# Gate transposes one token block later, pooling sums one group later, weights one block sooner, in a hybrid mLSTM encoder block

## The chip, the cores and the metric

The kernel runs on one core of one Trainium2 chip. The metric is the device time of one execution in microseconds (us). Five engines work side by side, each through its own queue in order: TensorE (PE, with its weight loads as PEld), VectorE (DVE), ScalarE (ACT), GpSimd (POOL) and SyncE (SP), which issues nearly all of the DMA transfers of the stretch in question.

## What is computed

One encoder block: a modulated RMSNorm, one input projection, an mLSTM scan in both directions over four heads, a multi-scale pooling group beside it, an output projection, and a squared-ReLU MLP. The change lies in the projection of the four pooling groups and of the gates. Of the reference, what matters here:

```python
proj = jnp.einsum('bsd,dp->bsp', h, w_in)                 # 2048 tokens x 2576 columns
q, k, v, o, gates, u = jnp.split(proj, cuts, axis=-1)     # u: 4 pooling groups of 128 channels
log_i = gates[:, 0] + b_igate[:, None, :, None]
log_f = jax.nn.log_sigmoid(gates[:, 1] + b_fgate[:, None, :, None])
b = jnp.cumsum(lf, axis=-1)                               # in each chunk of 128 tokens
m_new = jnp.maximum(b_last + m, jnp.max(g, axis=-1))      # running maximum over the 16 chunks
for gi, win in enumerate((2, 4, 8, 16)):                  # centred means of u, less the token itself
    means.append((p[:, hi] - p[:, lo]) / cnt[None, :, None])
mixed = jnp.stack(means, axis=2) - uf
mod = silu(c) @ w_ada + b_ada                             # 6 x 1024 modulation values
```

## The kernel before

Activations lie transposed in SBUF, 8 tiles of 128 channels by 512 tokens for each of four token blocks, split into a high and a low part (`Hh`, `Hl`). A column block of 128 output channels and 512 tokens is 24 matmuls (`col_mm`, lines 404 to 406: high by high, low by high, high by low, over 8 tiles of channels). In the text such a block is called c15_0: column block 15, token block 0.

The stage in question runs from about 134 us to 262 us. It goes over the pooling groups g = 3, 2, 1, 0 (column blocks 15, 14, 13, 12), four token blocks each. Five kinds of work are woven into it:

- **The gates** (`gate_rows`, a generator that is advanced once per token block by `next(gates, None)`): transposes of small matrices on TensorE, called gT, gL, gM, gC and gD by their PSUM tiles, with scans and copies on VectorE and exponentials on ScalarE between them. gL needs `g_last` from VectorE (lines 329 to 332), gM the rows of the running maximum (lines 342 to 349), gC the exponentials (lines 366 to 371), gD the decay (line 383).
- **Weights** (`col_weights`): a 512 KB load `wr`, a cast `wh` on ScalarE, and the low part `wl` on VectorE. They are asked for when token block 1 of the group before has been computed.
- **Pooling** (lines 445 to 458): after the four blocks of a group have been copied to `u`, VectorE forms the sums in one tile `s` with a single buffer: log2(window) additions over some 2050 columns, two small corrections and a subtraction; then four stores `yd` of 256 KB each. The next group's first sum overwrites `s`, so that it waits for those stores.
- **Folding of the output weights**: a 512 KB load `wor`, a scaling on VectorE (line 462), two matmuls `wof` (line 465), two copies and stores.
- **Modulation values** (`mod_col`): for each of 32 columns a 512 KB load `ada` and a multiply-and-sum on VectorE (line 117).

The loads `wr`, `wor` and `ada` share three buffers (`raw`); a load is issued when the tile that holds its buffer has been read for the last time, and SyncE issues loads and stores strictly in its own order. When the stage ends, head 0's keys follow: projections c4_3 to c4_0, each copied (`k`, line 486), transposed (`kn`), scaled (`kb`, `kf`, lines 497 and 498), and multiplied with values loaded from memory (`va`, line 484; `kvb`, line 508). The tiles of this part lie where the pooling tiles were, so `kb` and the load `va` wait for the last group's stores.

The order of instructions on each engine is made by a scheduler from the order of the program and readiness; `tc.keep_in_program_order(ins)` holds an instruction to its place in the program.

Of the kernel before, what the change touches and what calls it, by code (L numbers as in the profile page):

```python
# [8 lines left out]
F32 = mybir.dt.float32  # L9
# [3 lines left out]
ALU = mybir.AluOpType  # L13
# [13 lines left out]
WIN = (2, 4, 8, 16)  # L27
# [8 lines left out]
def block_kernel(ctx, tc, x, x_t, cb, w_ada, b_ada, g_mix, g_ffn, g_head, p_scale, w_col, w_vg,  # L36
# [273 lines left out]
    def gate_rows(pg):  # L310
        def gt(name, n=P):
            return pg.tile([P, n], F32, name=name)
        li, lf, b_, m_, t0 = gt("g_li"), gt("g_lf"), gt("g_b"), gt("g_m"), gt("g_t")
        ps = tp("gT")
        pe.transpose(ps[:, 0:P], G2[:, 0], ident)
        pe.transpose(ps[:, P:2 * P], G2[:, 1], ident)
        ve.tensor_scalar(li, ps[:, 0:P], bgate[:, 0:1], None, ALU.add)
        ve.tensor_scalar(lf, ps[:, P:2 * P], bgate[:, 1:2], None, ALU.add)
        sc.activation(t0, lf, AF.Abs)
        sc.activation(t0, t0, AF.Exp, scale=-1.0)  # L320
        sc.activation(t0, t0, AF.Ln, bias=1.0)
        ve.scalar_tensor_tensor(lf, lf, 0.0, t0, ALU.min, ALU.subtract)
        fw, bw = slice(0, 64), slice(64, 128)
        ve.tensor_tensor_scan(b_[fw], ones[fw], lf[fw], 0.0, ALU.mult, ALU.add)
        ve.tensor_tensor_scan(b_[bw, ::-1], ones[bw], lf[bw, ::-1], 0.0, ALU.mult, ALU.add)
        ve.tensor_tensor_scan(m_[fw], lf[fw], li[fw], NEG, ALU.add, ALU.max)
        ve.tensor_tensor_scan(m_[bw, ::-1], lf[bw, ::-1], li[bw, ::-1], NEG, ALU.add, ALU.max)
        lasts = gt("g_last", 2)
        ve.tensor_copy(lasts[fw, 0:1], b_[fw, P - 1:P])
        ve.tensor_copy(lasts[bw, 0:1], b_[bw, 0:1])  # L330
        ve.tensor_copy(lasts[fw, 1:2], m_[fw, P - 1:P])
        ve.tensor_copy(lasts[bw, 1:2], m_[bw, 0:1])
        yield
        ps = tp("gL")
        pe.transpose(ps[0:1, 0:P], lasts[:, 0:1], ident)
        pe.transpose(ps[0:1, P:2 * P], lasts[:, 1:2], ident)
        rows = pg.tile([1, 4, P], F32, name="g_rows")
        ve.tensor_copy(rows[:, 0:2, :], ps[0:1, 0:2 * P].rearrange("p (a n) -> p a n", a=2))
        gp.memset(rows[:, 3, :], 0.0)
        for h in range(H):  # L340
            r = slice(h * NT, (h + 1) * NT)
            ve.tensor_tensor_scan(rows[:, 2, r], rows[:, 0, r], rows[:, 1, r], 0.0, ALU.add, ALU.max)
            r = slice(64 + h * NT, 64 + (h + 1) * NT)
            ve.tensor_tensor_scan(rows[:, 2, r][:, ::-1], rows[:, 0, r][:, ::-1],
                                  rows[:, 1, r][:, ::-1], 0.0, ALU.add, ALU.max)
        r2 = rows[:, 2, :].rearrange("p (d h c) -> p d h c", d=2, h=H)
        r3 = rows[:, 3, :].rearrange("p (d h c) -> p d h c", d=2, h=H)
        ve.tensor_copy(r3[:, 0, :, 1:NT], r2[:, 0, :, 0:NT - 1])
        ve.tensor_copy(r3[:, 1, :, 0:NT - 1], r2[:, 1, :, 1:NT])
        yield  # L350
        ps = tp("gM")
        pe.transpose(ps[:, 0:1], rows[:, 3, :], ident[0:1, 0:1])
        mp = gt("g_mp", 1)
        ve.tensor_copy(mp, ps[:, 0:1])
        ve.scalar_tensor_tensor(m_, b_, mp, m_, ALU.add, ALU.max)
        u = lf
        v = li
        ve.tensor_tensor(v, li, b_, ALU.subtract)
        ve.tensor_tensor(u, b_, m_, ALU.subtract)
        for d in range(2):  # L360
            dma(ua_d[:, 0, d, :], u[64 * d:64 * d + 64])
        ul = gt("g_ul", 1)
        ve.tensor_copy(ul[fw], u[fw, P - 1:P])
        ve.tensor_copy(ul[bw], u[bw, 0:1])
        a = t0
        sc.activation(a, u, AF.Exp, bias=mp)
        for d in range(2):
            dma(ua_d[:, 1, d, :], a[64 * d:64 * d + 64])
        wk = b_
        sc.activation(wk, v, AF.Exp, bias=ul)  # L370
        sc.activation(m_, m_, AF.Exp, scale=-1.0)
        ve.tensor_copy(ul[fw], a[fw, P - 1:P])
        ve.tensor_copy(ul[bw], a[bw, 0:1])
        yield
        ps = tp("gC")
        pe.transpose(ps[:, 0:P], v, ident)
        pe.transpose(ps[:, P:2 * P], wk, ident)
        pe.transpose(ps[:, 2 * P:3 * P], m_, ident)
        ve.tensor_copy(vcol, ps[:, 0:P])
        ve.tensor_copy(wkcol, ps[:, P:2 * P])  # L380
        ve.tensor_copy(emcol, ps[:, 2 * P:3 * P])
        dd = gt("g_dd")
        ve.tensor_scalar(dd, ident, ul, None, ALU.mult)
        yield
        ps = tp("gD")
        pe.matmul(ps[:, 0:P], ones, dd, start=True, stop=True)
        ve.tensor_copy(decb, ps[:, 0:P])


    def col_weights(ci):  # L390
        r = raw(f"wr{ci}").rearrange("p (k n) -> p k n", k=KT)
        dma(r, w_col[ci])
        hh = wq.tile([P, KT, P], F32R, tag="whi", name=f"wh{ci}")
        hl = wq.tile([P, KT, P], F32R, tag="wlo", name=f"wl{ci}")
        sc.copy(hh, r)
        ve.tensor_tensor(hl, r, asf(hh), ALU.subtract)  # L396
        return hh, hl
# [17 lines left out]
    with tc.tile_pool(name="pu", bufs=2) as pu, tc.tile_pool(name="psU", bufs=2, space=PSUM) as psU:  # L415
        wpl = pu.tile([P, 4, P], F32, name="wpl", bufs=1)
        dma(wpl, w_pool)
        edgec = pu.tile([P, 64], F32, name="edgec", bufs=1)
        dma(edgec, edge)
        pgs = ExitStack()  # L420
        pg = pgs.enter_context(tc.tile_pool(name="pg", bufs=1))
        gates = gate_rows(pg)
        w = col_weights(15)
        for g in (3, 2, 1, 0):
            win = WIN[g]
            hw = win // 2
            u = pu.tile([P, T + 16], F32, tag="u", name=f"u{g}")
            gp.memset(u[:, 0:8], 0.0)
            gp.memset(u[:, T + 8:T + 16], 0.0)
            for b in range(NB):  # L430
                cg = col_mm(12 + g, b, w)
                while True:
                    try:
                        next(cg)
                    except StopIteration as e:
                        ps = e.value
                        break
                if b or g < 3:
                    next(gates, None)
                sc.copy(u[:, 8 + 512 * b:8 + 512 * b + 512], ps)  # L440
                if b == 1:
                    wn = col_weights(11 + g if g else 4)
            w = wn

            s = pu.tile([P, T + 16], F32, tag="s", name=f"s{g}", bufs=1)
            n = T + 15
            ve.tensor_tensor(s[:, 0:n], u[:, 0:n], u[:, 1:n + 1], ALU.add)
            d = 2
            while d < win:
                n -= d  # L450
                ve.tensor_tensor(s[:, 0:n], s[:, 0:n], s[:, d:n + d], ALU.add)
                d *= 2
            s = s[:, 8 - hw:8 - hw + T]
            ve.tensor_tensor(s[:, 0:8], s[:, 0:8], edgec[:, 16 * g:16 * g + 8], ALU.mult)
            ve.tensor_tensor(s[:, T - 8:T], s[:, T - 8:T], edgec[:, 16 * g + 8:16 * g + 16], ALU.mult)
            ve.scalar_tensor_tensor(s, s, 1.0 / win, u[:, 8:8 + T], ALU.mult, ALU.subtract)
            for b in range(NB):
                dma(y_d[b][:, 4 + g, :], s[:, 512 * b:512 * b + 512])

            wr = raw(f"wor{g}")  # L460
            dma(wr, w_o[4 + g])
            ve.tensor_scalar(wr, wr, pscale[:, g:g + 1], None, ALU.mult)
            for n in range(2):
                ps = psU.tile([P, 512], F32, tag="y", name=f"wof{g}_{n}")
                pe.matmul(ps, wpl[:, g], wr[:, 512 * n:512 * n + 512], start=True, stop=True)
                e = evt(f"woe{g}_{n}")[:, :512]
                sc.copy(e, ps)
                dma(wo_d[g][:, 512 * n:512 * n + 512], e)
            for j in MODS[g]:
                mod_col(j)  # L470
        pgs.close()
        for k in range(KT):
            ve.scalar_tensor_tensor(s2[:, k:k + 1], mod[:, 32 + k:33 + k], 1.0, gffn[:, k:k + 1],
                                    ALU.add, ALU.mult)


    with tc.tile_pool(name="ps_", bufs=2) as sp, tc.tile_pool(name="psS", bufs=1, space=PSUM) as psS:
# [223 lines left out]
        for h in range(H):  # L701
# [5 lines left out]
            n = 0  # L707
# [563 lines left out]
```

## Time and profile before

| | us |
|---|---|
| median of 3 runs | 2036.94 (2034.96 to 2037.42) |
| the profiled execution | 2039.14 |
| its span in the profile | 2037.1 |
| mean granted TensorE clock | 0.997 of full speed |

The profiled execution is 2.0 us longer than the span that the profile shows and 2.2 us above the median. All times in the rows are counted from the start of the span. A row of a timeline gives start, duration, engine, line, operation, tiles and shapes, how many alike, and in brackets how long the engine had been idle before and what ended that.

### The profile page before, as it was taken

The page shows a single profiled execution, that of the slowest core. Times are in us where ns is not written, and L with a number is a line of the kernel's source. Part 1 is how long each engine was busy: PE and PEld are TensorE (multiplying, and loading weights), DVE is VectorE, ACT ScalarE, POOL GpSimd, SP SyncE. Part 2 cuts the span into 40 slices and gives each one's busy share as a digit, 9 for nine tenths or more (in the row PEclk, how much of TensorE's full clock was granted, in tenths as well). Part 3 has the DMA queues.
Part 4 walks back from the last instruction along what each step waited for, and adds up shares of the span by engine and source line. Part 5 has one row for each costly group of instructions (what it writes and reads, how often), then busy time and mean ns, then how long its engine had stood idle before and what let it go on. Part 6 is the DMA issues. An engine that isn't in the chain of part 4 may idle for free.

```text
span 2037.1 us, 27780 instructions
## 1 busy us (share of the span) xinstructions
PE 1987.5 (98%) x9591; PEld 1658.5 (81%) x9591; DVE 1356.5 (67%) x2456; ACT 918.3 (45%) x1704; POOL 129.7 (6%) x353
## 2 busy tenths in 40 slices
PE   7999999989999999999999999999999999999998
PEld 6997777778887888888888888888888888888886
DVE  6638636676646777555666766666877667768876
ACT  4721223333335668755556655556324224324432
POOL 1100012222210111000000000000000000000011
PEclk9999999999999999999999999999999999999999
DMA  8736867787548799765666766766887657648553
GB/s 339 237 108 209 285 205 220 253 254 226 180 131 271 236 270 315 209 196 182 224 203 224 228 226 215 226 206 225 280 268 257 225 156 262 224 158 275 187 165 132
DMA packets 298574, 452.87 MB, mean 222 GB/s; under 512 B 23569, under 2 KB 163137, under 8 KB 298306
## 3 DMA queue, kind: packets, MB, share of 16 engines
q1 hardware_dynamic: 228546, 413.35, 62.3%
q10 hardware_dynamic: 69888, 37.76, 6.1%
q8 instruction: 75, 1.23, 0.2%
q14 instruction: 65, 0.53, 0.1%
HBM read 290.40 MB, written 160.62 MB: 221 GB/s over the span
## 4 chain that ended last, share of the span: by engine, by line
PE 84%; DMA 7%; DVE 4%; issue 1%; ACT 1%; POOL 1%; SPq 1%; POOLq 0%; DVEq 0%; ACTq 0%
PE c L405 4%; PE c L404 4%; PE c L406 4%; DMA ua<-uad 1%; DMA ada<-in_w_ada 1%; DVE ada L117 1%; DMA wotd<-os 1%; DMA rob<-wotd 1%; DMA vraw<-in_w_v 1%; PE f000x L845 1%; PE o11x L845 1%; PE o10x L845 1%; PE o13x L845 1%; PE o03x L845 1%; PE o12x L845 1%
## 5 line engine op out<-in xcount | busy, mean ns | idle before, releaser
L404 PE MATMUL c<-Hh,wh 128*128 128x512 f32 x512 | 211.0, 412 | 0.0
L405 PE MATMUL c<-Hl,wh 128*128 128x512 f32 x512 | 203.4, 397 | 0.0
L406 PE MATMUL c<-Hh,wl 128*128 128x512 f32 x512 | 202.8, 396 | 0.5 <-DVE wl L396 0.5
L406 PEld LDWEIGHTS c<-Hh,wl 128*128 128x128 f32 x512 | 96.6, 189 | 20.5 <-DVE wl L396 0.9
L404 PEld LDWEIGHTS c<-Hh,wh 128*128 128x128 f32 x512 | 97.0, 189 | 17.3 <-issue 1.0
L405 PEld LDWEIGHTS c<-Hl,wh 128*128 128x128 f32 x512 | 97.1, 190 | 16.8 <-issue 0.7
L117 DVE SCALAR_TENSOR_TENSOR ada<-ada,c_bc 128x1024 f32<-128x1024 f32 x48 | 58.1, 1221 | 22.4 <-DMA ada<-in_w_ada 22.3
L581 ACT ACTIVATE ua<-ua,vcol 128x128 f32<-128x128 f32 x64 | 25.7, 401 | 103.2 <-POOL ua L577 103.1
L780 ACT CAST wb<-rwb 128x1024 fp32r<-128x1024 f32 x56 | 58.7, 1051 | 26.0 <-DMA rwb<-twd 25.8
L961 POOL TENSOR_TENSOR g300ss<-g300ss 128x1 f32<-128x1 f32 x2 | 0.9, 451 | 1079.9 <-ACT g300j L957 1079.9
L783 DVE TENSOR_TENSOR wb<-rwb,wb 128x1024 fp32r<-128x1024 f32 x56 | 68.3, 1219 | 0.8 <-ACT wb L780 0.7
L622 ACT ACTIVATE jk<-hm 128x128 bf16<-128x128 f32 x64 | 19.6, 307 | 83.0 <-DVE hm L620 82.3
L586 DVE TENSOR_TENSOR ua<-ua,q 128x256 f32<-128x256 f32 x64 | 26.4, 425 | 37.5 <-DMA ua<-uad 26.8
L577 POOL TENSOR_SCALAR_AFFINE_SELECT ua<-ua 128x128 f32<-128x128 f32 x64 | 26.6, 416 | 270.7 <-DMA ua<-uad 135.4
L625 DVE TENSOR_TENSOR hm<-hm,hss 128x256 f32<-128x256 f32 x32 | 14.7, 458 | 38.9 <-POOL hss L129 38.9
L255 PE MATMUL vgp<-vgh,Hh 128*128 128x272 f32 x128 | 38.2, 301 | 2.3 <-ACT Hh L208 2.3
L440 ACT COPY u<-c 128x512 f32<-128x512 f32 x16 | 9.4, 585 | 63.7 <-PE c L406 59.4
L783 DVE TENSOR_TENSOR ob<-rob,ob 128x1024 fp32r<-128x1024 f32 x14 | 17.1, 1224 | 30.5 <-ACT ob L780 29.9
L256 PE MATMUL v2p<-v2h,Hh 128*128 128x256 f32 x128 | 36.2, 286 | 1.1 <-ACT v2h L236 1.1
L257 PE MATMUL vgp<-vgl,Hh 128*128 128x272 f32 x128 | 37.2, 292 | 0.0
L259 PE MATMUL vgp<-vgh,Hl 128*128 128x272 f32 x128 | 37.0, 294 | 0.0
L585 DVE TENSOR_TENSOR ua<-ua,S 128x256 f32<-128x256 f32 x64 | 26.5, 413 | 14.9 <-PE S L584 14.7
(4048 smaller groups left out, 6071.3 us busy)
## 6 DMA issues: line engine op xcount, KB each, us to landing
rwb<-twd SPq DMA_DIRECT2D x56, 512.0 KB, 6.1
ada<-in_w_ada SPq DMA_DIRECT2D x48, 512.0 KB, 5.2
ua<-uad SPq DMA_DIRECT2D x64, 256.0 KB, 4.1
j<-in_w SPq DMA_DIRECT2D x32, 512.0 KB, 5.4
twd<-t SPq DMA_DIRECT2D x64, 256.0 KB, 3.0
twd<-j SPq DMA_DIRECT2D x48, 256.0 KB, 2.8
wr<-in_w_col SPq DMA_DIRECT2D x16, 512.0 KB, 4.9
q<-qkd SPq DMA_DIRECT2D x32, 256.0 KB, 3.6
```

The lines of the kernel that those rows point to most:

```text
L117: ve.scalar_tensor_tensor(w, w, 1.0, c_bc, ALU.mult, ALU.mult, accum_out=mod[:, j:j + 1])
L255: pe.matmul(pa[:, :VG], hh, vgh[k], start=st, stop=False)
L256: pe.matmul(pb[:, :256], hh, v2h[k], start=st, stop=False)
L257: pe.matmul(pa[:, :VG], hh, vgl[k], start=False, stop=False)
L259: pe.matmul(pa[:, :VG], hl, vgh[k], start=False, stop=en)
L404: pe.matmul(ps, hh[:, k], Hh[b][:, k], start=k == 0, stop=False)
L405: pe.matmul(ps, hh[:, k], Hl[b][:, k], start=False, stop=False)
L406: pe.matmul(ps, hl[:, k], Hh[b][:, k], start=False, stop=k == KT - 1)
L577: gp.affine_select(W[:, 0], W[:, 0], pattern=[[1, P]], compare_op=ALU.is_ge, fill=NEG, base=0, channel_multiplier=-1)
L780: sc.copy(dst, src)
L783: ve.tensor_tensor(dst, src, asf(hi), ALU.subtract)
L845: pe.matmul(ps, a[:, k], b[:, k], start=start and k == 0 and n == 0, stop=k == 3 and n == 2, skip_group_check=not start)
```

## The change

Three things are moved; no arithmetic is added or taken away.

- In `gate_rows` a second `yield` stands ahead of gL, so that gL, gM, gC and gD come one token block later; the first transposes of gL, gM and gC are held to their place.
- The pooling of group g becomes a function `pooled`, called after token block 1 of the next group (for g = 0 after its own last block), its first addition held to its place.
- `col_weights` for the next group is called after token block 0 instead of 1.

```diff
         ve.tensor_copy(lasts[bw, 1:2], m_[bw, 0:1])
         yield
+        yield
         ps = tp("gL")
-        pe.transpose(ps[0:1, 0:P], lasts[:, 0:1], ident)
+        tc.keep_in_program_order(pe.transpose(ps[0:1, 0:P], lasts[:, 0:1], ident))
...
-        pe.transpose(ps[:, 0:1], rows[:, 3, :], ident[0:1, 0:1])
+        tc.keep_in_program_order(pe.transpose(ps[:, 0:1], rows[:, 3, :], ident[0:1, 0:1]))
...
-        pe.transpose(ps[:, 0:P], v, ident)
+        tc.keep_in_program_order(pe.transpose(ps[:, 0:P], v, ident))
...
+        us = []
+        def pooled(g, u):
+            win = WIN[g]
+            hw = win // 2
+            s = pu.tile([P, T + 16], F32, tag="s", name=f"s{g}", bufs=1)
+            n = T + 15
+            ins = ve.tensor_tensor(s[:, 0:n], u[:, 0:n], u[:, 1:n + 1], ALU.add)
+            tc.keep_in_program_order(ins)
...
+            for b in range(NB):
+                dma(y_d[b][:, 4 + g, :], s[:, 512 * b:512 * b + 512])
...
-                if b == 1:
+                if b == 0:
                     wn = col_weights(11 + g if g else 4)
+                if b == 1 and g < 3:
+                    pooled(g + 1, us.pop(0))
             w = wn
-            s = pu.tile([P, T + 16], F32, tag="s", name=f"s{g}", bufs=1)
...
+            us.append(u)
+            if g == 0:
+                pooled(0, us.pop(0))
```

What the scheduler makes of it is seen in three places. The numbers in the names tell tiles apart; lines of the changed kernel lie up to 11 lower.

TensorE around gL, before:

```order
L405 MATMUL c15_2_1667<-Hl2_745,wh15_1579 128x512
L406 MATMUL c15_2_1667<-Hh2_744,wl15_1580 128x512
L335 MATMUL gL_1692<-ident_78,g_last_1655 1x128
L336 MATMUL gL_1692<-ident_78,g_last_1655 1x128
L404 MATMUL c15_3_1709<-Hh3_1052,wh15_1579 128x512
```

and now:

```order
L406 MATMUL c15_3_1693<-Hl3_1053,wh15_1579 128x512
L407 MATMUL c15_3_1693<-Hh3_1052,wl15_1580 128x512
L336 MATMUL gL_1718<-ident_78,g_last_1661 1x128
L337 MATMUL gL_1718<-ident_78,g_last_1661 1x128
L476 MATMUL wof3_0_1738<-wor3_1735,wpl_1570 128x512
```

gL has moved behind c15_3; likewise gM now stands behind c14_0, gC behind c14_1 and gD behind c14_2.

VectorE between gM and gC, before (`g_ul` from `g_lf` feeds the exponential that gC waits for):

```order
L117 SCALAR_TENSOR_TENSOR ada45_1807,mod_90<-ada45_1807,c_bc_87 128x1024
L354 COPY g_mp_1736<-gM_1734 128x1
L123 TENSOR_TENSOR mod_90<-mod_90,bada_200 128x1
L355 SCALAR_TENSOR_TENSOR g_m_1640<-g_b_1639,g_mp_1736,g_m_1640 128x128
L117 SCALAR_TENSOR_TENSOR ada46_1811,mod_90<-ada46_1811,c_bc_87 128x1024
L359 TENSOR_TENSOR g_lf_1638<-g_b_1639,g_m_1640 128x128
```

and now:

```order
L117 SCALAR_TENSOR_TENSOR ada47_1784,mod_90<-ada47_1784,c_bc_87 128x1024
L123 TENSOR_TENSOR mod_90<-mod_90,bada_200 128x1
L355 COPY g_mp_1818<-gM_1816 128x1
L356 SCALAR_TENSOR_TENSOR g_m_1646<-g_b_1645,g_mp_1818,g_m_1646 128x128
L397 TENSOR_TENSOR wl13_1839<-wr13_1836,wh13_1838 128x1024
L360 TENSOR_TENSOR g_lf_1644<-g_b_1645,g_m_1646 128x128
```

The low part of the next weights, wl13, now stands ahead of `g_lf`, and the sums of ada46 and ada47 ahead of `g_mp`.

VectorE at the end of the stage, up to the first scaled keys `kb0_3`, before:

```order
L117 SCALAR_TENSOR_TENSOR ada17_2315,mod_90<-ada17_2315,c_bc_87 128x1024
L454 TENSOR_TENSOR s0_2289<-s0_2289,edgec_1572 128x8
L455 TENSOR_TENSOR s0_2289<-s0_2289,edgec_1572 128x8
L123 TENSOR_TENSOR mod_90<-mod_90,bada_200 128x1
L117 SCALAR_TENSOR_TENSOR ada18_2319,mod_90<-ada18_2319,c_bc_87 128x1024
L456 SCALAR_TENSOR_TENSOR s0_2289<-s0_2289,u0_2176 128x2048
L123 TENSOR_TENSOR mod_90<-mod_90,bada_200 128x1
L117 SCALAR_TENSOR_TENSOR ada19_2323,mod_90<-ada19_2323,c_bc_87 128x1024
L123 TENSOR_TENSOR mod_90<-mod_90,bada_200 128x1
L396 TENSOR_TENSOR wl0_2347<-wr0_2344,wh0_2346 128x1024
L497 TENSOR_TENSOR kb0_3_2396<-kn0_3_2390,wkcol_1561 128x512
```

and now:

```order
L117 SCALAR_TENSOR_TENSOR ada17_2315,mod_90<-ada17_2315,c_bc_87 128x1024
L442 SCALAR_TENSOR_TENSOR s1_2227<-s1_2227,u1_1997 128x2048
L123 TENSOR_TENSOR mod_90<-mod_90,bada_200 128x1
L117 SCALAR_TENSOR_TENSOR ada18_2319,mod_90<-ada18_2319,c_bc_87 128x1024
L117 SCALAR_TENSOR_TENSOR ada19_2323,mod_90<-ada19_2323,c_bc_87 128x1024
L123 TENSOR_TENSOR mod_90<-mod_90,bada_200 128x1 x2
L397 TENSOR_TENSOR wl0_2347<-wr0_2344,wh0_2346 128x1024
L432 TENSOR_TENSOR s0_2289<-u0_2166 128x2063
L440 TENSOR_TENSOR s0_2289<-s0_2289,edgec_1572 128x8
L441 TENSOR_TENSOR s0_2289<-s0_2289,edgec_1572 128x8
L442 SCALAR_TENSOR_TENSOR s0_2289<-s0_2289,u0_2166 128x2048
L508 TENSOR_TENSOR kb0_3_2396<-kn0_3_2390,wkcol_1561 128x512
```

The end of group 1's pooling (s1) has come into this stretch, and the whole of group 0's (s0) stands behind the sums of ada18 and ada19 and behind wl0, right ahead of `kb0_3`.

## Rows read from the trace of the kernel before

**Rows 1.** The page: busy time, share and instructions of each engine.

```profile
PE 1987.5 (98%) x9591; PEld 1658.5 (81%) x9591; DVE 1356.5 (67%) x2456; ACT 918.3 (45%) x1704; POOL 129.7 (6%) x353
```

**Rows 2.** What TensorE waited for, 134 to 265 us: total us, times, longest.

```profile
PE gL L335 <- issue: 4.1, 1, 4.1
...
PE wof L465 <- DVE wor L462: 0.9, 2, 0.8
PE c L406 <- DVE wl L396: 0.5, 1, 0.5
```

**Rows 3.** Timeline of TensorE around gL: start us, us, instruction, idle before.

```profile
149.30 0.39 PE L405 MATMUL c<-Hl,wh 128*128 128x512 f32 x1
...
150.89 0.39 PE L406 MATMUL c<-Hh,wl 128*128 128x512 f32 x1
155.34 0.27 PE L335 MATMUL gL<-ident,g_last 128*1 128x128 f32 x1 [4.06 <-issue]
156.25 0.63 PE L405 MATMUL c<-Hl,wh 128*128 128x512 f32 x1
...
159.12 0.39 PE L406 MATMUL c<-Hh,wl 128*128 128x512 f32 x1
```

**Rows 4.** Stretches: busy us of PE, PEld, DVE, ACT, POOL; granted clock; DMA share; GB/s.

```profile
155.60:158.80 3.20, 3.16 (x9) 2.48 (x9) 3.17 (x10) 0.00 (x0) 0.00 (x0) 0.50 0.24 44
253.00:257.00 4.00, 3.00 (x16) 2.16 (x15) 0.83 (x2) 0.00 (x0) 0.00 (x0) 1.00 0.94 315
```

**Rows 5.** Timeline of VectorE between gL and gM.

```profile
155.45 0.15 DVE L332 COPY g_last<-g_m 64x1 f32<-64x1 f32 x1
...
158.53 0.17 DVE L342 TENSOR_TENSOR_SCAN g_rows<-g_rows 1x16 f32<-1x16 f32 x1
...
160.55 1.23 DVE L117 SCALAR_TENSOR_TENSOR ada<-ada,c_bc 128x1024 f32<-128x1024 f32 x1 [0.95 <-DMA ada<-in_w_ada]
```

**Rows 6.** Timeline of ScalarE, the exponentials ahead of gC.

```profile
165.70 1.28 ACT L366 ACT_TABLE_LOAD   x1
...
167.50 0.40 ACT L370 ACTIVATE g_b<-g_li,g_ul 128x128 f32<-128x128 f32 x1
```

**Rows 7.** Groups of VectorE, 134 to 262 us: busy us, mean ns, idle before, releaser.

```profile
L117 DVE SCALAR_TENSOR_TENSOR ada<-ada,c_bc 128x1024 f32<-128x1024 f32 x32 | 38.9, 1221 | 16.8 <-DMA ada<-in_w_ada 16.7
L447 DVE TENSOR_TENSOR s<-u 128x2063 f32<-128x2063 f32 x4 | 9.2, 2303 | 0.2 <-ACT u L440 0.2
...
L396 DVE TENSOR_TENSOR wl<-wr,wh 128x1024 fp32r<-128x1024 f32 x5 | 6.1, 1224 | 5.9 <-ACT wh L395 5.9
```

**Rows 8.** Timeline of VectorE, from group 1's folding to the first scaled keys.

```profile
211.91 0.75 DVE L462 TENSOR_SCALAR wor<-wor,pscale 128x1024 f32<-128x1024 f32 x1
...
235.06 1.23 DVE L396 TENSOR_TENSOR wl<-wr,wh 128x1024 fp32r<-128x1024 f32 x1 [0.77 <-ACT wh L395]
236.31 0.75 DVE L462 TENSOR_SCALAR wor<-wor,pscale 128x1024 f32<-128x1024 f32 x1
...
239.41 2.31 DVE L447 TENSOR_TENSOR s<-u 128x2063 f32<-128x2063 f32 x1
241.63 0.15 DVE L123 TENSOR_TENSOR mod<-mod,bada 128x1 f32<-128x1 f32 x1
...
252.25 0.69 DVE L497 TENSOR_TENSOR kb<-kn,wkcol 128x512 f32<-128x512 f32 x1 [2.23 <-DMA yd<-s]
```

**Rows 9.** Issues on SyncE; then issue to landing of the ada loads (134 to 262 us).

```profile
247.34 1.79 SPq L458 DMA_DIRECT2D yd<-s  x4
252.20 0.33 SPq L484 DMA_DIRECT2D va<-vd  x1
...
DMA to landing us min/median/max: 3.3/4.3/6.3
```

**Rows 10.** Timeline of TensorE at the first products of the keys.

```profile
255.84 0.46 PE L508 MATMUL kvb<-va,kb 128*128 128x129 f32 x2 [1.00 <-DMA wr<-in_w_col]
262.14 0.55 PE L491 MATMUL kn<-ident,k 128*128 128x128 f32 x3 [1.21 <-ACT k L486]
```

More of the change, by code (lines that the diff above doesn't have):

```diff
@@ L422, in block_kernel @@
         gates = gate_rows(pg)
+        us = []
[6 more added lines that the diff above has]
+            tc.keep_in_program_order(ins)
+            d = 2
+            while d < win:
+                n -= d
+                ve.tensor_tensor(s[:, 0:n], s[:, 0:n], s[:, d:n + d], ALU.add)
+                d *= 2
+            s = s[:, 8 - hw:8 - hw + T]
+            ve.tensor_tensor(s[:, 0:8], s[:, 0:8], edgec[:, 16 * g:16 * g + 8], ALU.mult)
+            ve.tensor_tensor(s[:, T - 8:T], s[:, T - 8:T], edgec[:, 16 * g + 8:16 * g + 16], ALU.mult)
+            ve.scalar_tensor_tensor(s, s, 1.0 / win, u[:, 8:8 + T], ALU.mult, ALU.subtract)
+            for b in range(NB):
+                dma(y_d[b][:, 4 + g, :], s[:, 512 * b:512 * b + 512])
         w = col_weights(15)
         for g in (3, 2, 1, 0):
-            win = WIN[g]
-            hw = win // 2
             u = pu.tile([P, T + 16], F32, tag="u", name=f"u{g}")
@@ L440, in block_kernel @@
                 sc.copy(u[:, 8 + 512 * b:8 + 512 * b + 512], ps)
-                if b == 1:
+                if b == 0:
                     wn = col_weights(11 + g if g else 4)
+                if b == 1 and g < 3:
+                    pooled(g + 1, us.pop(0))
             w = wn
-            s = pu.tile([P, T + 16], F32, tag="s", name=f"s{g}", bufs=1)
[L446 to L458, printed above, removed]
+            us.append(u)
+            if g == 0:
+                pooled(0, us.pop(0))
             wr = raw(f"wor{g}")
```

## The prediction

> **What bounds the kernel now.** I began with the page's busy line: TensorE works in 1987.5 us of a span of 2037.1 [rows 1]. A change that adds no arithmetic can therefore win only where TensorE waits, or lose by a new wait of it. So I read next what it waited for in the stage that the diff touches. One wait stands out, 4.06 us ahead of gL; two weight waits are below 1 us [rows 2]. The timeline shows the place [rows 3], and the windows what it left behind: a granted clock of 0.50, the lower level of 1.2 GHz, over the next nine matmuls, whereas around a wait of 1.00 us it was 1.00 throughout [rows 4, 10]. Then I went over to VectorE, since every moved step lies on it or waits for it. It is not full: 16.8 us of its idle time in this stage wait for ada loads and 5.9 for casts [rows 7]. But at the end of the stage it stands on the path: the first `kb` waited 2.23 us for the stores `yd` of group 0 [rows 8], the load `va` went out just then [rows 9], and TensorE's first `kvb` followed 1.00 us late [rows 10]. This second place decides, I think, as the change puts more work ahead of those stores.
>
> **The gate wait goes.** A projection matmul starts every 0.227 us (149.30 to 150.89 is seven of them) [rows 3]. From 150.89 to 159.12, 8.23 us, TensorE got through nine such starts, 2.05, and two transposes, 0.2: the lost time is 6.0 us, 4.06 of it idle and the rest half clock. With gL behind c15_3, c15_3 ends near 156.6, while `g_last` was ready at 155.6 [rows 5]. A row with a 1 us margin and no matmul to spare: I take the full 6.0.
>
> **What waits in the gates now.** VectorE has more to do between the transposes. Behind gL it stands first at the sum of ada45, which was free at 161.7 [rows 5], then at ada46, whose load goes out when ada44 has been read (about 158.2) and takes 4.3 [rows 9]; with 1.2 for its sum, and 1.07 for scans and copies (158.53 to 159.60) [rows 5, 7], the rows for gM are ready at 164.7. TensorE arrives after gL, `wof3` (1.4) and c14_0 (24 x 0.227 = 5.5) at 164.1: it waits 0.6. Behind gM come ada47 (load from 161.8, read by 167.3), the weight load wr13 (163.7 + 4.7), its cast of 1.1 (5.9 us of waits for five `wl`) and wl13, 1.2 [rows 7]: 170.6. Only then `g_lf`, 0.3, and table load and exponentials, 165.70 to 167.90 before [rows 6]: 173.1. TensorE stands at gC from 170.4, so it waits 2.7. At the best (loads at 3.3) it waits at neither; at the worst (6.3) for 5 and with half clock. I take 3.3 together: the median landing is the row for loads that go out two or three abreast.
>
> **The pooling is late from the start.** Group 3's five operations on `s` take 5 x 2.2 (239.41 to 241.63 is one) [rows 8], with corrections 11.2, and are woven with four small gate copies, 0.8, and three sums, 3.6; begun at 173.6, behind the exponentials, they are done at 189.2. Its four stores need 1.79 to issue [rows 9] and stand on SyncE ahead of the load of ada34, which now goes out at about 191.5. Three loads abreast land after some 5.5, and the sum of ada35 ends at 199.6. That frees the buffer of wr12: landing 5.1, cast 1.1, wl12 1.2, to 206.9. Behind it VectorE does the first addition of group 2, held in its place, to 209, when the folding `wor1` can start: 208.8 against 211.91 [rows 8]. TensorE would be at `wof1` by 207.8 and waits 1, about what it waited at `wof` before [rows 2].
>
> **From group 1's folding to group 0's.** Before, 211.91 to 235.06 is 23.15 us [rows 8] and holds three operations on `s` and eight ada sums. It holds as many now, of other groups. Behind it stand the last `wl`, 1.15, the first addition of group 1, which is new there, 2.2, and `wor0`, 0.75: done at 208.8 + 27.2 = 236.0, against 237.06 [rows 8]. So VectorE is still 1 us ahead here, and TensorE is ahead too.
>
> **Then two poolings instead of one.** This is the term that costs. Behind `wor0` VectorE has group 1's second addition 2.2, ada16 1.15, corrections 0.25, ada17 1.15 and the subtraction 2.2: 7.0. Then group 1's stores go out; before, four issues began at 247.34 and the waiting `kb` started at 252.25, so stores cost 4.9 [rows 8, 9]. Group 0's first addition needs `s` free, so the stores would hold it to 11.9; beside them run ada18, ada19 and the cast and low part of the next weights, which hold VectorE to 11.75 by their loads: no extra. It starts at 12.2, and with 2.2, 0.25 and 2.2 the subtraction ends at 16.85. Group 0's stores, 4.9 to 5.0, are landed at 236.0 + 21.9 = 257.9; before it was 252.2 [rows 8]. Bounds: no wait for loads and stores of 4 us give 254; each of the three last landings at the longest of [rows 9], 6.3 for 4.3, gives 262.
>
> **What that does to TensorE.** `kb` and `va` wait for these stores as before, for the tiles lie there. From 252.20 to `kvb` at 255.84 was 3.6 [rows 9, 10]: now 261.5. TensorE, without its old loss, is there at 254.4, with nothing behind `kvb` that it may take first: it idles for 7 us. From 252.20 to `kn` at 262.14 was 9.94 [rows 9, 10]; two exponentials of 0.40 [rows 6] more ahead of the copy of `k`, and `ua` loads half a microsecond sooner, leave 10.1: 268.0. Five more matmuls, 1.14, lie behind TensorE by then. So the kernel is later by 268.0 - 1.14 - 262.14 = 4.7 us. The gain of 6.0 and the gate waits do not enter: TensorE comes to this wait earlier or later and leaves it at the same moment. What follows has the order of before, with TensorE 98% busy [rows 1], so 4.7 stays to the end.
>
> The half clock after 7 us idle (shown after 4.06 of idle time) [rows 3, 4] costs 1.3 to 1.7 where matmuls follow one another (seven starts took 2.87 there and not 1.6), but here the products of the keys wait for VectorE between them and for `kn` anyway; I take 0, and 1.7 as the other end.
>
> **A rule beside the rows.** The landings of the loads carry the sum, 4.3 at the median [rows 9]. The Trainium skill, DMA: Bandwidth & Descriptors, section "Anatomy of one DMA — SWDGE (gpsimd) path", gives for one transfer, issued by GpSimd, about 2.0 us plus its bytes at 436 GB/s. As an estimate from that page, 512 KB would take 3.2 us and 256 KB 2.6. Only the minimum of the trace agrees (3.3), so the median decides; by the page's figures the chain, with its five exposed landings 1.1 to 2.3 shorter each, would end some 8 us sooner, near 250, at the edge between the first and the second rival below.
>
> **The sum.** The profiled execution was 2039.14, 2.0 outside its span of 2037.1, and 2.2 above the median 2036.94. The difference of 4.7 applied to the profiled run gives 2043.8, and to the median 2041.6, which I predict.
>
> **Rivals.** (a) *Faster*: landings near the minimum of 3.3 [rows 9] all along. The chain to the last stores holds about 12 us of waits for transfers; if these shrink so far that the stores land before 249, TensorE no longer waits at `kvb` and the gate gain shows: -6.0, +0.6 and 1 to 2.7 for gM, gC and `wof1`, less some 2 of removed waits [rows 2, 10], -5 to -6 in all, or 2031 to 2032. Against it: in this stage the loads stand abreast, and the median is 1 us above the minimum. (b) *No change*: stores land between 249.1 and 257.3 (4.1 us, 0.2%, about what a measurement of this kernel can tell from no change, on either side of 253.2, where the old loss and the new one are equal), 2033 to 2041. Each landing 0.5 us shorter than I took is enough for it. VectorE's 16.8 us of waiting for ada loads [rows 7] speaks for it, since part of the moved work may fall into them. (c) *Costlier*: two of the last landings at 6.3, or the half clock not hidden: +6 to +9, 2043 to 2046. (d) That the change doesn't do what it says is excluded by the order: gL stands behind c15_3, and the weights are asked for sooner.
>
> **How the numbers follow.** My forecast, group 0's stores landed between 257.3 and 260, has 0.39; (c) has 0.15; together slower by over 0.2%: 0.54. (b) has 0.38, (a) 0.08. The range leaves out (a), half of which lies below 2032, and the lower edge of (b), and most of what lies beyond (c): 2035.0 to 2046.0. Of that, slower alone is 2041 to 2046.
>
> **What the profile after would show.** No idle time ahead of gL and clock 1.00 from 155 to 159. Short waits at gM and gC, the latter 2 to 3, released by ScalarE. `wor1` starting at 207 to 211, VectorE's second operation on group 1 behind `wor0`, `kb` waiting on `yd` and starting near 258 instead of 252.25, TensorE idle for 5 to 8 us at `kvb`, released by the load `va`. I am wrong if `kb` starts before 253 (then the weights, asked for sooner, drew the chain forward), if gC waits over 4 us, or if TensorE finds other matmuls to do ahead of `kvb`.

## The result, and the profile after

| | before | after |
|---|---|---|
| median of 6 runs each, us | 2037.62 (2034.96 to 2042.8) | 2051.0 (2046.89 to 2054.52) |
| after to before | | 1.0052 (1.0038 to 1.0066) |
| profiled execution, span, us | 2037.1 | 2049.2 |

The change makes the kernel slower by 0.52%, 7.7 to 13.4 us by the interval; the two medians lie 13.4 us apart, at its upper edge. Forecast were 4.7 us and at most 2046: the direction and the place were right, the size was not.

TensorE has as many instructions and as much to do as in [rows 1]:

```profile
PE 1988.8 (97%) x9591; PEld 1659.7 (81%) x9591; DVE 1357.4 (66%) x2456; ACT 917.8 (45%) x1704; POOL 131.2 (6%) x353
```

What TensorE waited for from 134 to 275 us (total us, times, longest), to be read beside [rows 2]:

```profile
PE kvb L519 <- issue: 7.2, 1, 7.2
PE wof L476 <- DVE wor L473: 3.5, 2, 2.9
PE gC L378 <- ACT g_b L371: 3.3, 1, 3.3
PE gM L353 <- DVE g_rows L350: 1.0, 1, 1.0
PE kn L502 <- ACT k L497: 1.0, 1, 1.0
```

The wait ahead of gL is gone. In its place stand three waits further on, and then the long one ahead of the first `kvb`. The stretches (us of PE, PEld, DVE, ACT, POOL; then granted clock) show gL's place, the place of gM and gC, and the matmuls behind `kvb`:

```profile
155.60:158.80 3.20, 3.20 (x13) 1.98 (x12) 1.78 (x7) 1.76 (x3) 0.00 (x0) 1.00 0.59 172
164.00:176.00 12.00, 8.69 (x39) 6.94 (x40) 8.01 (x17) 4.18 (x7) 0.00 (x0) 1.00 0.71 250
...
262.00:266.00 4.00, 1.84 (x7) 1.62 (x7) 0.88 (x2) 0.00 (x0) 0.00 (x0) 0.50 0.92 296
266.00:270.00 4.00, 4.00 (x19) 3.22 (x19) 2.03 (x5) 0.17 (x1) 0.50 (x2) 0.83 0.93 233
```

Where nine matmuls ran at 0.50 [rows 4], thirteen now run at 1.00. VectorE's timeline from the folding of group 1 to the first scaled keys (start us, us, instruction, idle before), which answers to [rows 8]:

```profile
210.58 0.75 DVE L473 TENSOR_SCALAR wor<-wor,pscale 128x1024 f32<-128x1024 f32 x1
...
237.61 0.75 DVE L473 TENSOR_SCALAR wor<-wor,pscale 128x1024 f32<-128x1024 f32 x1
...
243.00 2.29 DVE L442 SCALAR_TENSOR_TENSOR s<-s,u 128x2048 f32<-128x2048 f32 x1
...
252.00 2.31 DVE L432 TENSOR_TENSOR s<-u 128x2063 f32<-128x2063 f32 x1 [1.71 <-DMA yd<-s]
...
261.30 0.69 DVE L508 TENSOR_TENSOR kb<-kn,wkcol 128x512 f32<-128x512 f32 x1 [4.39 <-DMA yd<-s]
```

The row at 243.00 is group 1's subtraction; group 0's first addition follows only at 252.00, released by group 1's stores, and `kb` only at 261.30 (252.25 before), released by group 0's. On SyncE the four stores of group 1, of group 0, and the load `va` (compare [rows 9]):

```profile
245.32 2.28 SPq L444 DMA_DIRECT2D yd<-s  x4
...
256.93 1.79 SPq L444 DMA_DIRECT2D yd<-s  x4
261.13 0.80 SPq L495 DMA_DIRECT2D va<-vd  x2
```

And TensorE at its first products of the keys (compare [rows 10]):

```profile
264.16 0.77 PE L519 MATMUL kvb<-va,kb 128*128 128x129 f32 x2 [7.17 <-issue]
...
271.47 0.55 PE L502 MATMUL kn<-ident,k 128*128 128x128 f32 x3 [0.99 <-ACT k L497]
```

`kn` starts 9.3 us later than before; with the 1.14 of matmuls that are behind TensorE by then, the kernel is 8.2 us late here. This execution was 1.0 us ahead when the gates began, by the last copy of `g_last` (155.45 before [rows 5]):

```profile
154.47 0.15 DVE L332 COPY g_last<-g_m 64x1 f32<-64x1 f32 x1
```

Counted from that copy, in what I call the clock of the stage, it is 9.2 us late at `kn`.

### The profile page after: what moved, and what is told of

The parts are those of the page before. It is cut to its first block, busy times and chain, and to the rows that moved or that the text cites. A ratio compares the mean times of both kernels' runs of the same rounds, so it can differ in the third digit from the quotient of the medians.

```text
span 2049.2 us, 27782 instructions
## 1 busy us (share of the span) xinstructions
PE 1988.8 (97%) x9591; PEld 1659.7 (81%) x9591; DVE 1357.4 (66%) x2456; ACT 917.8 (45%) x1704; POOL 131.2 (6%) x353
## 4 chain that ended last, share of the span: by engine, by line
PE 83%; DMA 7%; DVE 6%; ACT 1%; issue 1%; POOL 1%; SPq 1%; POOLq 0%; DVEq 0%; ACTq 0%
PE c L406 3%; PE c L405 3%; PE c L407 3%; DMA ua<-uad 2%; DVE ada L117 2%; DMA ada<-in_w_ada 2%; DMA wr<-in_w_col 1%; DMA wotd<-os 1%; DMA vraw<-in_w_v 1%; PE f000x L856 1%; PE o11x L856 1%; PE o13x L856 1%; PE o10x L856 1%; PE o12x L856 1%; PE o03x L856 1%
## 5 line engine op out<-in xcount | busy, mean ns | idle before, releaser
L117 DVE SCALAR_TENSOR_TENSOR ada<-ada,c_bc 128x1024 f32<-128x1024 f32 x48 | 58.1, 1221 | 27.8 <-DMA ada<-in_w_ada 27.7
L519 PEld LDWEIGHTS kvb<-va,kb 128*128 128x128 f32 x120 | 20.4, 193 | 24.5 <-issue 7.5
L519 PE MATMUL kvb<-va,kb 128*128 128x129 f32 x120 | 25.7, 296 | 14.8 <-issue 7.2
```

Source lines behind the costliest of these rows:

```text
L117: ve.scalar_tensor_tensor(w, w, 1.0, c_bc, ALU.mult, ALU.mult, accum_out=mod[:, j:j + 1])
L519: pe.matmul(kvj, kb[:, j], vt[:, j], start=True, stop=True)
```

## The experiments

Theory A: the loss is made at the end of the stage, where group 1's and group 0's poolings stand behind one another on VectorE and `kb` and `va` wait for the last stores. Rival B: the gate steps make it, by their new waits at gM, gC and `wof1`. Rival C: the weights, asked for sooner, take a load buffer from the ada loads. Each kernel is compared with runs of the kernel before on the same chip, by their ratio (the kernel before had medians of 2042 to 2043 there). The whole change was not run again beside them. "First result" is the start of the scan's first `jk` on ScalarE; the last three columns come from one profiled execution each. The last `g_last` stands between 153.2 and 157.2, and 1.6 us apart (154.5 to 156.1) in kernels that differ only far behind it, so most of this is chance. To compare two rows, take their difference in `g_last` off first.

| kernel | ratio (95% interval) | last `g_last` | `kb` starts | first result |
|---|---|---|---|---|
| before | 1 | 155.5 | 252.3 | 295.7 |
| all of the change | 1.0052 (1.0038 to 1.0066) | 154.5 | 261.3 | 303.8 |
| gates alone | 1.0009 (0.9998 to 1.0019) | 157.2 | 255.7 | 302.2 |
| pooling alone | 1.0041 (1.0027 to 1.0055) | 156.9 | 265.3 | 308.0 |
| all, but group 1's pooling at its own end | 1.0004 (0.9995 to 1.0014) | 154.6 | 255.4 | 296.3 |
| all, `kb` and `va` freed of the stores | 1.0028 (1.0015 to 1.0040) | 156.1 | 256.3 | 302.1 |
| all, group 0's sums not in `s` | 1.0032 (1.0016 to 1.0049) | 155.7 | 257.7 | 301.7 |
| all, but weights as before | 1.0041 (1.0026 to 1.0057) | 154.4 | 260.2 | 302.7 |
| gates, group 3's pooling, `kb` freed | 1.0011 (1.0001 to 1.0022) | 155.1 | 250.3 | 297.5 |
| the same, `g_lf` ahead of wl13 | 1.0026 (1.0013 to 1.0040) | 156.8 | 252.4 | 305.7 |
| all, eight ada sums written later | 0.9997 (0.9988 to 1.0006) | 157.1 | 250.3 | 299.2 |
| the same, `kb` and `va` freed | 1.0005 (0.9995 to 1.0015) | 153.2 | 243.3 | 293.7 |
| before, eight ada sums written later | 0.9986 (0.9977 to 0.9996) | 155.9 | 251.6 | 294.3 |
| gates, group 3's pooling, `kb` freed, eight sums later | 1.0001 (0.9989 to 1.0012) | 154.2 | 249.8 | 296.9 |

**The gates alone.**

```diff
         yield
+        yield
         ps = tp("gL")
-        pe.transpose(ps[0:1, 0:P], lasts[:, 0:1], ident)
+        tc.keep_in_program_order(pe.transpose(ps[0:1, 0:P], lasts[:, 0:1], ident))
...
```

(gM and gC are held alike, as in the change.)

> Only the gate part of the change: gL, gM, gC and gD one token block later and held to their place; pooling and weights as before. Theory A (the loss of the change comes from the stores of group 0, which land at 261 instead of 252 because two poolings stand behind one another at the end of the stage): group 0's sums stand where they stood before or sooner, so TensorE must not wait 7 us at its first kvb; the 6 us of gL come back, less new waits at gM and gC, because group 3's five sums are now woven between the gates' copies: 5 to 9 us of such waits, so 2034 to 2041. Rival B (the loss comes from the gate steps themselves, which wait 1.0, 3.3 and 2.9 us at gM, gC and wof1 in the changed kernel): 2045 to 2051, with the wait at kvb as long as in the changed kernel.

Measured: 1.0009, 2 us and not clearly different from none. What TensorE waited for from 134 to 275 us, and the first `kb` on VectorE:

```profile
PE gM L353 <- DVE g_rows L350: 4.9, 1, 4.9
PE c L405 <- ACT wh L396: 2.2, 2, 1.6
PE kvb L509 <- DMA kwd<-kf: 1.2, 1, 1.2
```

```profile
255.70 0.69 DVE L498 TENSOR_TENSOR kb<-kn,wkcol 128x512 f32<-128x512 f32 x1 [2.20 <-DMA yd<-s]
```

The wait has moved from gL to gM, since two of group 3's additions (165.35 and 168.26 on VectorE) now stand among the steps that form `g_rows`; gC is no longer waited for, `c` waits 2.2 for weights, and `kvb` only 1.2 us. So the gate steps don't make the loss, but alone they gain nothing either.

**The pooling alone.**

```diff
+                if b == 1 and g < 3:
+                    pooled(g + 1, us.pop(0))
...
-            ve.tensor_tensor(s[:, 0:n], u[:, 0:n], u[:, 1:n + 1], ALU.add)
...
+            us.append(u)
+            if g == 0:
+                pooled(0, us.pop(0))
```

> Only the pooling part: the sums of a group behind token block 1 of the next, group 0's at its own end; gates and weights as before. Theory A: the end of the stage has the order of the changed kernel (group 1's sums behind wor0, then its stores, then group 0's sums, then kb), so group 0's stores land at 258 to 262 and TensorE leaves its first kvb as late as in the changed kernel: 2045 to 2051, whether gL waits before or not. Rival B (gate steps): gates stand as before and VectorE has fewer sums among them, so 2033 to 2038.

Measured: 1.0041, some 8 us. The waits of TensorE and the first `kb`:

```profile
PE kvb L518 <- issue: 8.0, 1, 8.0
PE gL L335 <- issue: 4.5, 1, 4.5
PE wof L475 <- DVE wor L472: 2.7, 2, 2.4
```

```profile
265.26 0.69 DVE L507 TENSOR_TENSOR kb<-kn,wkcol 128x512 f32<-128x512 f32 x1 [4.38 <-DMA yd<-s]
```

This part alone brings 8 of the 10.6 us (the intervals overlap) with the same wait at `kvb`, though gL waits as before. B falls. `kb` is 4 us later than in the changed kernel, but this execution was 2.4 us later when the gates began (156.9 against 154.5); where the other 1.6 come from isn't shown.

**Group 1's pooling at its own end**, all else of the change kept.

```diff
-                if b == 1 and g < 3:
+                if b == 1 and 0 < g < 3:
                     pooled(g + 1, us.pop(0))
...
-            if g == 0:
-                pooled(0, us.pop(0))
+            if g < 2:
+                pooled(g, us.pop(0))
```

> The changed kernel with one thing undone: group 1's pooling stands at the end of group 1 again, so that only group 0's sums are left behind wor0. Gates, weights and the pooling of groups 3 and 2 stay changed. Theory A: group 0's stores land at 250 to 254, TensorE waits 0 to 3 us at its first kvb, and the time is 2033 to 2040. Rival B (gate steps, which are untouched here): no gain, 2047 to 2052. A third possibility, that the three stores of 2, 1 and 0 only shift the delay to wor1 or wl4: 2042 to 2047 with a longer wait at wof.

Measured: 1.0004, no different from before; the intervals of this kernel and of the whole change don't touch. The waits, and VectorE's start of group 0's sums and of `kb`:

```profile
PE wof L476 <- DVE wor L473: 4.5, 2, 3.5
PE gC L378 <- ACT g_b L371: 2.6, 1, 2.6
PE kvb L519 <- issue: 1.4, 1, 1.4
PE c L407 <- DVE wl L397: 1.0, 1, 1.0
```

```profile
245.00 2.31 DVE L432 TENSOR_TENSOR s<-u 128x2063 f32<-128x2063 f32 x1 [1.20 <-DMA yd<-s]
...
255.44 0.69 DVE L508 TENSOR_TENSOR kb<-kn,wkcol 128x512 f32<-128x512 f32 x1 [1.08 <-DMA yd<-s]
```

The wait at `kvb` is 1.4 instead of 7.2, and with it the loss is gone. (The profiled execution took 2039.0, where the median of this kernel is 2042.5.) `kb` came a little later than I expected (255.4, not 250 to 254), and the gain of gL still doesn't show: `wof` waits 4.5 and gC 2.6.

**`kb` and `va` freed of the stores.** `s` gets a pool of its own, and so do `va` and `kb`:

```diff
+            tc.tile_pool(name="py", bufs=1) as py:
...
-            s = pu.tile([P, T + 16], F32, tag="s", name=f"s{g}", bufs=1)
+            s = py.tile([P, T + 16], F32, tag="s", name=f"s{g}", bufs=1)
...
+    with tc.tile_pool(name="pk", bufs=2) as pk, tc.tile_pool(name="ps_", bufs=2) as sp,
...
-                vt = sp.tile([P, 4, 129], F32, tag="va", name=f"va{h}_{b}", bufs=2)
+                vt = pk.tile([P, 4, 129], F32, tag="va", name=f"va{h}_{b}", bufs=2)
...
```

> The changed kernel with the tile s in a pool of its own and va and kb in a pool that only takes the place of the other pooling tiles, so that kb and va wait for group 0's last sum but no longer for its stores. Theory A: kb starts right behind the last sum, at 257 instead of 261.3; TensorE's first kvb comes 3.5 to 4.5 us sooner, with a shorter half clock behind it: 2045 to 2048, 4 to 6 us less than the changed kernel. Rival B (gate steps): no difference from the changed kernel, 2049 to 2052. If the load va, which stands behind the four stores on SyncE, takes the place of the stores as what kvb waits for, the gain is 2 to 3 us.

Measured: 1.0028, some 6 us of loss instead of 10.6 (the intervals just meet). `kb` starts without a wait, and TensorE's waits at `kvb` are short:

```profile
256.29 0.69 DVE L509 TENSOR_TENSOR kb<-kn,wkcol 128x512 f32<-128x512 f32 x1
```

```profile
PE kvb L520 <- DVE kb L509: 1.9, 1, 1.9
...
PE kvb L520 <- DMA va<-vd: 0.6, 1, 0.6
PE kvb L520 <- DVE Cb L525: 0.4, 1, 0.4
```

So, by the middle values, about half of the loss hung on the stores through `kb` and `va`. By the order in which the tiles are declared `kb` should lie where `u1` was, not `s`; then it waited for the stores from `s` because new tiles wait for the whole pool whose place they take. The traces show no addresses, so this is argued, not shown. The other half of the loss stays: in the clock of the stage, the scan's first result comes 3.3 us sooner than in the changed kernel, but still 5.8 later than before; the tiles of the scan still take the place of `s`. That this is why it stays is argued from the columns of the table, not shown.

**Group 0's sums in the buffer of `u1`.**

```diff
-            s = pu.tile([P, T + 16], F32, tag="s", name=f"s{g}", bufs=1)
+            s = pu.tile([P, T + 16], F32, tag="s" if g else "u", name=f"s{g}", bufs=1 if g else 2)
```

> The changed kernel with group 0's sums in the free buffer of u1 instead of in s, so that its first sum doesn't wait for the four stores of group 1; the order of poolings stays stacked. Theory A, with the term that was short in the sum (in the changed kernel group 0's first sum began 6.8 us after group 1's last one ended, waiting for those stores): group 0's first sum starts at 246 to 248 instead of 252, its stores land at 257 to 258 instead of 261, and the loss shrinks from 10.6 us to 6 to 8 (ratio to the kernel before 1.003 to 1.004). Rival B (gate steps): the loss stays at 8 to 13 us (1.004 to 1.0065). A third possibility, that the stores of both groups then share the transfer engines and land as late as before: 1.005.

Measured: 1.0032, the foreseen value, though its interval overlaps that of the whole change. On VectorE, group 1's subtraction, group 0's first addition and subtraction, and `kb`:

```profile
242.39 2.29 DVE L442 SCALAR_TENSOR_TENSOR s<-s,u 128x2048 f32<-128x2048 f32 x1
...
245.81 2.30 DVE L432 TENSOR_TENSOR s<-u 128x2063 f32<-128x2063 f32 x1
...
250.60 2.29 DVE L442 SCALAR_TENSOR_TENSOR s<-s,u 128x2048 f32<-128x2048 f32 x1
...
257.72 0.69 DVE L508 TENSOR_TENSOR kb<-kn,wkcol 128x512 f32<-128x512 f32 x1 [4.83 <-DMA yd<-s]
```

Group 0's sums now start 1.2 us behind group 1's instead of 6.8, and `kb` is 3.6 us sooner (4.8 in the clock of the stage): in the trace the first round of stores was on the path, though the times alone don't tell this kernel from the whole change.

**Weights as before**, the rest changed.

```diff
-                if b == 0:
+                if b == 1:
                     wn = col_weights(11 + g if g else 4)
```

> The changed kernel with its third part undone: weights asked for behind token block 1 again. VectorE's order differs only around group 3's sums, which come ahead of the scaling wor2 and of the sums of ada28 to ada30. Theory A: this part has next to no share in the loss, since the end of the stage has the same order; group 3's stores go out 2 to 4 us sooner and wor1 follows 0 to 3 us sooner: 7 to 11 us slower than the kernel before (1.0035 to 1.0055). Rival C (the weights, asked for sooner, take a buffer that the ada loads needed, and that delays the whole chain): 0 to 4 us slower (1.000 to 1.002).

Measured: 1.0041; `kb` at 260.2 and TensorE's wait at `kvb` 7.4, as in the changed kernel. C falls.

**Group 3's pooling alone moved**, with the gates and with `kb` and `va` freed; then with `g_lf` held ahead of wl13.

```diff
-                if b == 1 and g < 3:
-                    pooled(g + 1, us.pop(0))
+                if b == 1 and g == 2:
+                    pooled(3, us.pop(0))
...
-            if g == 0:
-                pooled(0, us.pop(0))
+            if g < 3:
+                pooled(g, us.pop(0))
```

> A version that keeps what gained and leaves out what lost: the gates one token block later, only group 3's pooling moved into the next group (so that its sums don't stand among the gate copies), the poolings of 2, 1 and 0 at the end of their own group, and kb and va freed of group 0's stores by pools of their own. Theory A: the 6 us of gL come back less 1 at gM, 3 at gC and 0 to 1 at wof1, and kvb waits for nothing: 1 to 3 us faster than the kernel before (0.9985 to 0.9995). Rival B: the gate steps cost more than gL gave, 2 to 6 us slower (1.001 to 1.003).

```diff
-        ve.tensor_tensor(u, b_, m_, ALU.subtract)
+        tc.keep_in_program_order(ve.tensor_tensor(u, b_, m_, ALU.subtract))
...
-        ve.tensor_tensor(hl, r, asf(hh), ALU.subtract)
+        ins = ve.tensor_tensor(hl, r, asf(hh), ALU.subtract)
+        if ci == 13:
+            tc.keep_in_program_order(ins)
```

> The version before it, with g_lf and the low part wl13 held to the order of the program, so that wl13 no longer stands ahead of g_lf. Theory A: the wait at gC, 3.3 us in the changed kernel, falls to 0 to 1, so 3 to 5 us faster than the kernel before (0.9975 to 0.9985), unless the time is given back at the next wait for VectorE (wof1 or kvb), which would leave it where the version before it stands.

Measured: 1.0011 and 1.0026; both miss, and the second is the worse one. Its waits of TensorE from 134 to 275 us, and the stretch behind the longest:

```profile
PE c L407 <- ACT wh L396: 5.2, 2, 4.5
PE gC L378 <- ACT g_b L371: 1.6, 1, 1.6
```

```profile
214.00:230.00 16.00, 15.39 (x51) 10.84 (x51) 12.29 (x21) 1.76 (x3) 0.00 (x0) 0.79 0.81 279
```

gC's wait did fall, from 3.0 in the first of the two (3.3 in the changed kernel) to 1.6. But the weights of a later group came 4.5 us too late, with half clock behind the wait (mean 0.79). This profiled execution took 2055.5, where the median of the kernel is 2047.8, so the 4.5 may be more than is usual. I put that wait down to wl13, which now stands further back and frees its load buffer later; this link is read from the order and wasn't tried by itself. What is taken from one wait in this stage comes back at the next one.

**Eight ada loads and sums written later**, behind head 0's first projections, for the changed kernel, for the same with `kb` and `va` freed, for the kernel before, and for the version with only group 3's pooling moved.

```diff
-MODS = (range(16, 20), range(20, 28), range(28, 38), range(38, 48))
+MODS = (range(24, 28), range(28, 34), range(34, 40), range(40, 48))
+TAIL = range(16, 24)
...
         for _ in qk_proj(0, Cb):
             pass
+        for j in TAIL:
+            mod_col(j)
```

> The changed kernel, with its stacked poolings, and the loads and sums of ada16 to ada23 taken out of the stage: they are written behind head 0's first projections, the other 24 spread 8, 6, 6, 4 over the groups instead of 10, 10, 8, 4. Theory A, sharpened by the runs so far (what sets the time of group 0's stores is VectorE's chain through the three load buffers): about 8 x 1.2 us of sums and eight loads less stand ahead of the stores, so they land 6 to 9 us sooner, at 252 to 255; the wait at gC falls too, since g_mp no longer stands behind two sums; the loss of 10.6 us goes to between -4 and +2 (ratio 0.998 to 1.001). If the chain is set by the poolings and stores alone, the stores land at 259 to 262 and the loss stays at 8 to 12.

> The version before it, with va and kb freed of group 0's stores by pools of their own. Theory A: TensorE's first kvb waits for nothing any more, and the 6 us of gL show, less about 1 at the gates and 1 at wof1: 2 to 5 us faster than the kernel before (0.9975 to 0.999). If the scan of head 0, whose first loads still wait for the stores, takes the place of kvb, no better than the version without the pools.

> The kernel before, with only ada16 to ada23 moved behind head 0's first projections and the other 24 spread as in the two versions above; gates, pooling and weights as before. Theory A: gL still waits 4 us and leaves the half clock; only the small waits go (wof 0.9, wl 0.5, kvb 1.0), so 0 to 2.5 us faster than the kernel before (0.999 to 1.000). What the two versions above gain over this one is then the gate part's own worth. Rival (the eight loads only move to a place where they collide with head 0's): 0 to 3 us slower.

> Gates one block later, only group 3's pooling moved, va and kb in pools of their own, and ada16 to ada23 moved behind head 0's first projections. Theory A: as the version with all poolings moved and pools of their own, since nothing is stacked here: 2 to 5 us faster than the kernel before (0.9975 to 0.999). If stacking still costs there, this one is the faster by the difference.

Measured: 0.9997, 1.0005, 0.9986 and 1.0001. In the traces the eight don't leave the stage altogether, as the scheduler draws them forward: the last sum starts between 261.7 and 270.0 (247.3 before). But ahead of group 0's last operation on `s` stand 24 of the 32 sums in the first two kernels, where all 32 stood in the changed one, and 26 in the other two (31 before). With the poolings stacked as in the change, but eight sums fewer ahead of them, the loss is gone and `kb` starts at 250.3:

```profile
250.31 0.69 DVE L509 TENSOR_TENSOR kb<-kn,wkcol 128x512 f32<-128x512 f32 x1 [1.38 <-DMA yd<-s]
```

TensorE still waits at its first `kvb`, but the wait ends at 254.99 and not at 264.16 (255.84 before), though this execution took 2046.9, where the median of the kernel is 2040.6:

```profile
254.99 0.77 PE L520 MATMUL kvb<-va,kb 128*128 128x129 f32 x2 [5.24 <-DVE mod L124]
```

So stacking is dear only with so much other work ahead of it. Whether VectorE's time, the three load buffers or the transfers are what is short, this edit doesn't tell, as it moves all of them at once. The best of all is the kernel before with this edit alone, faster than before by 0.04 to 0.23%, and it beats both kernels, though gL waits in it nearly as before:

```profile
PE gL L336 <- issue: 3.7, 1, 3.7
PE kvb L509 <- DMA va<-vd: 2.2, 2, 1.5
```

The three others, which have the gates moved, don't beat it; the expectations of 0.9975 to 0.999 for two of them failed. In none of the six kernels with late gates and repaired poolings did the 6 us of gL appear: TensorE's waits that the view lists from 134 to 275 us add up to 7.7 before, to between 7.9 and 11.3 in these six, and to 5.9 in the best version.

## Why the prediction was right in direction and wrong in size

- **The gate wait.** Gone, as forecast: no idle time ahead of gL, clock 1.00 there.
- **What waits in the gates now.** Forecast 0.6 at gM, 2.7 at gC and 1 at `wof1`; measured 1.0, 3.3 and 2.9. The first two were a little short, the third by 1.9; TensorE's own waits were not on the path that set the end, as it waited 7.2 at `kvb` afterwards. That this meets the forecast of 7 is luck: TensorE came to `kvb` at 257.0, not 254.4, and the stores were late by about as much. The rows behind gC show clock 1.00, so the 3.3 cost no half clock.
- **The pooling is late from the start.** This is the step that failed. `wor1` was forecast for 208.8 and started at 210.58. In this execution the stage ran ahead, too: the last `g_last` stood at 154.47 instead of 155.45 [rows 5], so the term was short by 2.8 in the clock of the stage. About half of it came from the gate steps: group 3's sums began 1.3 late in this clock (173.91 in the trace, forecast 173.6) and, as long as forecast, ended 1.4 late. The other half lies behind them: the four stores took 2.22 us on SyncE (1.79 taken), a `wod` store behind them 0.95 more, and the first load behind these landed 5.9 after its issue, where I had taken 5.5.
- **From group 1's folding to group 0's.** 27.7 for 27.2 (210.58 to 237.61, and 0.66): right.
- **Then two poolings instead of one.** Group 1's sums took 6.9 (forecast 7.0) behind `wor0`. I had let the stores run beside ada18, ada19 and the weights, and group 0's sums start 5.2 behind group 1's; they started 6.8 behind, released by the stores (the row at 252.00). The stores were what was mis-sized, and not the work beside them: from their first issue to their landing they took 6.7 (245.32 to 252.00), where I had put 4.9 from [rows 8, 9]. So the term came out 1.6 short, and the run with group 0's sums elsewhere showed that wait to be real. Group 0's own sums took 4.8 (4.65), its stores 4.3 (5.0).
- **The sum of these.** The stores were landed at 261.1 instead of 257.9, in the clock of the stage 4.2 later than forecast. My own upper bound for this time was 262. From there on the working held: `kvb` 3.0 behind them (forecast 3.6), `kn` 10.3 (10.1), and the half clock behind the wait (0.50, 0.83) didn't add to it.
- **From the stage to the kernel.** With the landing as measured, my own steps give 4.7 + 4.2 = 8.9 us, inside the measured 7.7 to 13.4. The range ended at 2046 because I let landings be long only at the end of the chain; a late first term and a second short one were enough to leave it. The bound of 262 was also added up too low: as written, three landings of 6.3 for 4.3 add 6.0 to 257.9, which is 263.9 and a time of 2047.6. What is left of the difference between 8.9 and the middle, 10.6, isn't settled; part of the profiled execution's 12.1 is chance (last section).
- **The rivals.** "No change" needed the stores at 257.3 or sooner; "faster" at 249. With the estimate from the Trainium skill, DMA: Bandwidth & Descriptors, section "Anatomy of one DMA — SWDGE (gpsimd) path", group 0's stores would have landed near 250; the trace says 261.1, and its ada loads took 4.4 at the median, so that here the skill's figure for GpSimd's transfers is too short for loads that go out several abreast from SyncE.
- **Who pays.** The prediction's claim that the gate gain doesn't enter, because TensorE meets the late stores anyway, held for the whole change. But the full 6.0 that I took for it, and that "faster" counted on, is in no run: with the gates alone, where `kvb` waits only 1.2, the wait came back as 4.9 at gM and 2.2 at `c`, and nothing was gained (1.0009). The pooling alone lost 8 us, and undoing group 1's part of it brought the time back.

## What to carry to other kernels

Where one engine sets the times at which another is released, removing a wait of the other engine may only move the wait along, as with gL here; the edit that paid was the one that put less work ahead of the releases (in its trace 26 sums instead of 31 ahead of group 0's last operation). A pooling step that is put off isn't free because its engine is only 67% busy: ask which stores and which buffer stand behind it, above all at the end of a stage where new tiles may wait for a whole pool. And where a forecast is a long chain of landings, let every one of them be late together for the upper bound.

## What the runs showed of the hardware

Far behind the changed part, where the output projection starts, TensorE waits once for a cast that waits for a load. TensorE's row and the stretch with its granted clock, in the kernel before:

```profile
646.65 0.73 PE L845 MATMUL o00x<-ob,o002h 128*128 128x512 f32 x2 [1.26 <-ACT o002h L780]
```

```profile
645.00:650.00 5.00, 3.02 (x12) 1.89 (x11) 4.86 (x8) 4.48 (x8) 0.00 (x0) 1.00 0.72 273
```

And in the changed kernel:

```profile
657.29 1.22 PE L856 MATMUL o00x<-ob,o002h 128*128 128x512 f32 x2 [2.89 <-ACT o002h L791]
```

```profile
655.00:660.00 5.00, 2.48 (x5) 1.57 (x6) 4.88 (x7) 4.29 (x8) 0.00 (x0) 0.65 0.80 302
```

A wait of 1.26 left the clock at 1.00, one of 2.89 was followed by matmuls at half clock, and the same matmuls that start 9.2 us later than before ahead of this place start 12.8 later behind it: 3.5 us from a wait that is 1.6 longer. Yet the length of the wait alone doesn't tell. With the gates and group 3's pooling moved and `kb` freed, a wait of 0.98 here was followed by half clock too, though TensorE's next wait, 0.7 us two matmuls later, was the same in it as in the kernel before:

```profile
647.90 0.73 PE L857 MATMUL o00x<-ob,o002h 128*128 128x512 f32 x2 [0.98 <-ACT o002h L792]
```

```profile
650.00:652.00 2.00, 2.00 (x7) 1.52 (x6) 2.00 (x4) 1.50 (x2) 0.00 (x0) 0.50 0.93 311
```

Waits of 1.50 here (the pooling alone) and of 3.3 at gC left it at 1.00. Half clock followed at this place in six of the fourteen profiled executions, that of the best version among them (a wait of 3.9, clock 0.50). It may account for a part of the spread of 2046.9 to 2054.5: the run of 2046.9 had a mean granted clock of 0.997, that of 2054.5 one of 0.993. The Trainium skill, TensorE: Matmul & The Clock Gate, Part 1, says that the point of transition varies because the activity is looked at in a window that runs freely; that a shorter wait was followed by half clock here and a longer one was not agrees with that.
